# A two-expert gate that writes 67 MB: the first store is issued from GpSimd's queue instead of ScalarE's

## The chip, the core and the metric

The kernel runs on one core of a Trainium2 chip. The metric is the device time of one execution in microseconds (us), taken as the median of several runs. The core has compute engines that matter here in three roles: VectorE (DVE) does the arithmetic, ScalarE (ACT) two small activations, and SyncE (SP), ACT and GpSimd (POOL) can each issue transfers between the chip's memory and the on-chip tiles. The transfers themselves are carried by the core's 16 DMA engines, whoever issued them.

## The reference

```python
def reference(x, router_logits, k):          # x: 16 x 1024 x 512, logits: 16 x 1024 x 8, k = 2
    logits_max = np.max(router_logits, axis=-1, keepdims=True)
    probs = np.exp(router_logits - logits_max)
    probs = probs / np.sum(probs, axis=-1, keepdims=True)
    topk_indices = np.argsort(probs, axis=-1)[..., -k:]
    topk_probs = np.take_along_axis(probs, topk_indices, axis=-1)
    topk_probs = topk_probs / np.sum(topk_probs, axis=-1, keepdims=True)
    x_expanded = x[:, :, np.newaxis, :].repeat(k, axis=2)
    return (x_expanded * topk_probs[..., np.newaxis]).astype(np.float32)
```

For each of 16,384 tokens the two largest of eight logits give two weights that add to one, and the token's 512 numbers are written out twice, once times each weight. The input is 33.6 MB of x and 0.5 MB of logits, the output 67.1 MB.

## The kernel before

The tokens are split into two groups of 128 x 65 and 128 x 63 (`GROUPS`): each of the 128 partitions holds 65, then 63 rows, a row being one token's 512 float32 numbers (2 KB in, 4 KB out). Three tiles matter. `xs` holds the loaded rows of a group. `osp` has room for 18 output rows a partition, and before that serves as scratch for the weights. `WA` holds the two weights of every token.

`LOADS` cuts the loading of a group into transfers of 2, 4, 28 and 31 rows a partition (group 0) and 16, 16 and 31 (group 1). `STORES` lists, for each group, the stores as (first row, number of rows, tile, place in the tile). A store of place "osp" is computed into `osp`; a store of place "xs" overwrites `xs` in place, since two output rows' worth of loaded rows have been used up by then. For every store one DVE multiplication (line 138) makes the product. Where the place in `osp` is used a second time in the group (`again`), the product is cut in two: the first `FREE[g]` rows, which lie where an earlier and smaller store was, and the rest, which lie where a larger one was.

```python
LOADS = [[2, 4, 28, 31], [16, 16, 31]]
STORES = [
    [(0, 3, "osp", 0), (3, 15, "osp", 3), (18, 16, "xs", 0), (34, 15, "osp", 0), (49, 16, "xs", 33)],
    [(0, 16, "osp", 2), (16, 16, "xs", 0), (32, 15, "osp", 0), (47, 16, "xs", 32)],
]
FREE = [3, 2]
```

The early store of the title is the first entry, `(0, 3, "osp", 0)`: three rows a partition, 12 KB in one piece for each partition, made as soon as the weights are there. Its place, rows 0 to 2 of `osp`, is written again by the first part of the product for `(34, 15, "osp", 0)`, which must wait until the early store has been read out. Below, the stores of group 0 are called the early store, store 2, store 3, store 4 and store 5, in the order of the list.

All transfers but the early store are issued by SP (lines 122, 130, 131 and 151), in the order written, which `tc.keep_in_program_order` fixes. SP's queue therefore holds, in this order: the loads of 2 and 4 rows, the two pieces of the logits, the loads of 28 and 31 rows, stores 2 to 5, and then the loads and stores of group 1. Each store waits in SP's queue for its product. The early store alone stands on another queue, ACT's, which after the two activations (lines 37 and 38) has nothing else to do. Line 155 puts an empty instruction on SP that waits for all but the last transfer.

Of the kernel before, what the change touches and what calls it, by code (L numbers as in the profile page):

```python
# [1 line left out]

# [4 lines left out]

F32 = mybir.dt.float32
ALU = mybir.AluOpType
ACTF = mybir.ActivationFunctionType  # L10
P = 128


def top2_weights(nc, WA, dlt, room, logits, E):

    tt = nc.vector.tensor_tensor
    hi, lo, n = None, None, E  # L20
    while n > 1:
        n //= 2
        if hi is None:
            a, b = logits[:, :, 0:n], logits[:, :, n : 2 * n]
            nhi, nlo = room(n), b
            tt(nhi, a, b, op=ALU.max)  # L26
            tt(nlo, a, b, op=ALU.min)  # L27
        else:
            a, b = hi[:, :, 0:n], hi[:, :, n : 2 * n]
            nhi, nlo, tmp = room(n), room(n), room(n)  # L30
            tt(tmp, lo[:, :, 0:n], lo[:, :, n : 2 * n], op=ALU.max)  # L31
            tt(nlo, a, b, op=ALU.min)  # L32
            tt(nlo, nlo, tmp, op=ALU.max)  # L33
            tt(nhi, a, b, op=ALU.max)  # L34
        hi, lo = nhi, nlo
    tt(dlt, hi[:, :, 0], lo[:, :, 0], op=ALU.subtract)  # L36
    nc.scalar.activation(WA[:, :, 0], dlt, ACTF.Sigmoid, scale=-1.0)  # L37
    return nc.scalar.activation(WA[:, :, 1], dlt, ACTF.Sigmoid, scale=1.0)  # L38

GROUPS = [65, 63]

LOADS = [[2, 4, 28, 31], [16, 16, 31]]
BASE = [0, 1]
# [6 lines that stand above are left out]
L = 18  # L52

FREE = [3, 2]


@with_exitstack
def kernel(
    ctx: ExitStack,
    tc: tile.TileContext,  # L60
    x: bass.AP,
    router_logits: bass.AP,
    k: bass.AP,
    out: bass.AP,
):
    nc = tc.nc
    B, S, D = x.shape
    E = router_logits.shape[-1]
    N = B * S
    assert int(k) == 2 and E == 8 and N == P * sum(GROUPS)  # L70
    M = N // P

    x_v, o_v, rl_v = [], [], []
    t0 = 0
    for n in GROUPS:
        t1 = t0 + P * n
        x_v.append(
            x.rearrange("b s d -> (b s) d")[t0:t1].rearrange("(p m) d -> p m d", p=P)
        )
        o_v.append(  # L80
            out.rearrange("b s k d -> (b s) k d")[t0:t1].rearrange(
                "(p m) k d -> p m k d", p=P
            )
        )
        rl_v.append(
            router_logits.rearrange("b s e -> (b s) e")[t0:t1].rearrange(
                "(p m) e -> p m e", p=P
            )
        )
        t0 = t1  # L90

    wpool = ctx.enter_context(tc.tile_pool(name="wpool", bufs=1))
    xs = wpool.tile([P, max(GROUPS), D], F32)
    osp = wpool.tile([P, L, 2, D], F32)
    WA = wpool.tile([P, M, 2], F32)
    dlt = wpool.tile([P, M], F32)


    flat = osp.rearrange("p l k d -> p (l k d)")
    taken = [0]  # L100

    def room(n):
        o = taken[0]
        taken[0] += M * n
        return flat[:, o : o + M * n].rearrange("p (m n) -> p m n", n=n)

    logits = room(E)

    def place(where, at, n):

        if where == "osp":
            return osp[:, at : at + n]
        return xs[:, at : at + 2 * n, :].rearrange("p (r k) d -> p r k d", k=2)

    moved = []
    m0 = 0
    for g, G in enumerate(GROUPS):
        x0, r = BASE[g], 0
        for n in LOADS[g]:
            moved.append(  # L120
                tc.keep_in_program_order(
                    nc.sync.dma_start(  # L122
                        xs[:, x0 + r : x0 + r + n, :], x_v[g][:, r : r + n, :]
                    )
                )
            )
            r += n
            if g == 0 and r == 6:
                n0 = GROUPS[0]
                tc.keep_in_program_order(nc.sync.dma_start(logits[:, :n0], rl_v[0]))  # L130
                tc.keep_in_program_order(nc.sync.dma_start(logits[:, n0:], rl_v[1]))  # L131
                weights = top2_weights(nc, WA, dlt, room, logits, E)
        assert r == G
        for r, n, where, at in STORES[g]:
            og = place(where, at, n)
            again = where == "osp" and at == 0 and r > 0
            for a, b in [(0, FREE[g]), (FREE[g], n)] if again else [(0, n)]:
                product = nc.vector.tensor_tensor(  # L138
                    og[:, a:b],
                    xs[:, x0 + r + a : x0 + r + b, :]  # L140
                    .unsqueeze(2)
                    .to_broadcast([P, b - a, 2, D]),
                    WA[:, m0 + r + a : m0 + r + b, :]
                    .unsqueeze(3)
                    .to_broadcast([P, b - a, 2, D]),
                    op=ALU.mult,
                )

            queue = nc.scalar if g == r == 0 else nc.sync
            moved.append(  # L150
                tc.keep_in_program_order(queue.dma_start(o_v[g][:, r : r + n], og))  # L151
            )
        m0 += G

    seen = tc.keep_in_program_order(nc.sync.nop())
    for ins in [weights, product] + moved[:-1]:
        tc.add_manual_dep(
            seen.ins,
            ins.ins.name,
            mybir.DependencyInfo(  # L160
                mybir.DependencyClass.Sync, mybir.DependencyReason.DATA
            ),
            reason="all but the last transfer is done",
        )


# [1 line left out]
_INS = ['x', 'router_logits', 'k']  # L168
_OUTS = [((16, 1024, 2, 512), 'float32')]

_NUMBERS = {'k': 2}


# [26 lines left out]
```

## Time and profile before

| what | us |
|---|---|
| runs | 240.18 median of 3 (239.93 to 241.43) |
| profiled execution, its own time | 241.36 |
| its span, first to last instruction | 239.6 |
| DVE busy | 141.9 |
| ACT busy | 1.8 |
| POOL busy | 0.2 |
| SP's queue (q1): packet time of the 16 DMA engines | 96.7% of the span |
| ACT's queue (q10): packet time of the 16 DMA engines | 1.5% of the span |

The profile comes as a page with sums and as views of the trace: the queues and their issues, the timeline, the chain of work that ended last, and the busy time in chosen stretches. A line of the timeline gives the start, the duration, the engine ("SPq" or "ACTq" is the issuing part of that engine), the source line, the operation, and what is written from what. In the issues, "us to landing" is the time from issue until the transfer's completion was signalled. The number of packets counts pieces that a DMA engine handles one after the other.

### The profile page before, as it was taken

The numbers are of one execution on the slowest core, as the hardware profiler recorded it, in microseconds if no ns is written. First come the engines' busy times: TensorE is split into PE (matmuls) and PEld (weight loads), VectorE is DVE, ScalarE is ACT, GpSimd is POOL, SyncE is SP. The second block draws the span as 40 slices with busy tenths as digits, with TensorE's granted clock in tenths as the row PEclk, the third lists the DMA queues.
The fourth block names the chain that finished last, engine by engine and source line by source line (L and its number), as shares of the span: only waits on it lengthen the run. The fifth ranks groups of instructions, "written<-read, shape, count | busy, mean of one in ns | idle before, by whom it ended". The sixth has DMA issues, their size and how long they took to land.

```text
span 239.6 us, 106 instructions
## 1 busy us (share of the span) xinstructions
DVE 141.9 (59%) x22; ACT 1.8 (1%) x3; POOL 0.2 (0%) x4
## 2 busy tenths in 40 slices
DVE  0560499999789999200000699999405999960000
ACT  2000000000000000000000000000000000000000
POOL 0000000000000000000000000000000000000000
DMA  7989998979989897999899999999999899898984
GB/s 253 528 373 483 427 415 376 493 339 492 481 372 492 383 482 339 482 437 449 361 421 438 438 438 498 435 419 471 405 405 471 372 503 442 380 492 360 514 350 186
DMA packets 2592, 101.19 MB, mean 422 GB/s; under 512 B 288, under 2 KB 416, under 8 KB 672
## 3 DMA queue, kind: packets, MB, share of 16 engines
q1 hardware_dynamic: 2448, 99.62, 96.7%
q10 hardware_dynamic: 144, 1.57, 1.5%
HBM read 34.08 MB, written 67.11 MB: 422 GB/s over the span
## 4 chain that ended last, share of the span: by engine, by line
DMA 48%; DVE 40%; SPq 1%; issue 0%; DVEq 0%
DMA xs<-in_x_dram 25%; DVE osp L138 25%; DMA out_dram<-osp 23%; DVE xs L138 14%; SPq L122 0%; SPq L131 0%; SPq L130 0%; SPq L151 0%; DVEq L138 0%
## 5 line engine op out<-in xcount | busy, mean ns | idle before, releaser
L138 DVE TENSOR_TENSOR osp<-xs,WA 128x3072 f32<-128x3072 f32 (+5 forms) x7 | 69.4, 9909 | 62.7 <-DMA xs<-in_x_dram 47.3
L138 DVE TENSOR_TENSOR xs<-xs,WA 128x16384 f32<-128x16384 f32 x4 | 68.9, 17224 | 0.1
L26 DVE TENSOR_TENSOR osp<-osp 128x512 f32<-128x512 f32 x1 | 0.7, 693 | 8.5 <-DMA osp<-in_router_logits_dram 8.5
L37 ACT ACT_TABLE_LOAD x1 | 1.3, 1283 | 0.7 <-PEq L181 0.7
L27 DVE TENSOR_TENSOR osp<-osp 128x512 f32<-128x512 f32 x1 | 0.7, 691 | 0.0
L32 DVE TENSOR_TENSOR osp<-osp 128x256 f32<-128x256 f32 (+1 forms) x2 | 0.7, 351 | 0.0
L31 DVE TENSOR_TENSOR osp<-osp 128x256 f32<-128x256 f32 (+1 forms) x2 | 0.7, 350 | 0.0
L34 DVE TENSOR_TENSOR osp<-osp 128x256 f32<-128x256 f32 (+1 forms) x2 | 0.7, 350 | 0.0
L33 DVE TENSOR_TENSOR osp<-osp 128x256 f32<-128x256 f32 (+1 forms) x2 | 0.7, 350 | 0.0
L37 ACT ACTIVATE WA<-dlt 128x128 f32<-128x128 f32 x1 | 0.3, 315 | 10.5 <-DVE dlt L36 10.5
L36 DVE TENSOR_TENSOR dlt<-osp 128x128 f32<-128x128 f32 x1 | 0.3, 292 | 0.0
L38 ACT ACTIVATE WA<-dlt 128x128 f32<-128x128 f32 x1 | 0.3, 297 | 0.0
L181 POOL MEMSET const-bfloat16-1.0<- 128x1 bf16 x1 | 0.1, 101 | 0.0
L181 POOL MEMSET const-uint8-127<- 128x1 uint8 x1 | 0.1, 101 | 0.0
L181 POOL MEMSET const-float32-0.0<- 128x1 f32 x1 | 0.1, 98 | 0.2 <-issue 0.2
L181 POOL MEMSET const-float32-1.0<- 128x1 f32 x1 | 0.1, 98 | 0.0
## 6 DMA issues: line engine op xcount, KB each, us to landing
out_dram<-osp SPq DMA_DIRECT2D x3, 7680.0 KB, 23.5
xs<-in_x_dram SPq DMA_DIRECT2D x2, 7936.0 KB, 42.2
xs<-in_x_dram SPq DMA_DIRECT2D x2, 4096.0 KB, 40.1
xs<-in_x_dram SPq DMA_DIRECT2D x1, 7168.0 KB, 24.8
out_dram<-osp ACTq DMA_DIRECT2D x1, 1536.0 KB, 26.6
xs<-in_x_dram SPq DMA_DIRECT2D x1, 1024.0 KB, 5.9
xs<-in_x_dram SPq DMA_DIRECT2D x1, 512.0 KB, 3.9
osp<-in_router_logits_dram SPq DMA_DIRECT2D x1, 260.0 KB, 6.2
```

The costliest lines, as they stand in the source:

```text
L26: tt(nhi, a, b, op=ALU.max)
L27: tt(nlo, a, b, op=ALU.min)
L31: tt(tmp, lo[:, :, 0:n], lo[:, :, n : 2 * n], op=ALU.max)
L32: tt(nlo, a, b, op=ALU.min)
L33: tt(nlo, nlo, tmp, op=ALU.max)
L34: tt(nhi, a, b, op=ALU.max)
L36: tt(dlt, hi[:, :, 0], lo[:, :, 0], op=ALU.subtract)
L37: nc.scalar.activation(WA[:, :, 0], dlt, ACTF.Sigmoid, scale=-1.0)
L38: return nc.scalar.activation(WA[:, :, 1], dlt, ACTF.Sigmoid, scale=1.0)
L138: product = nc.vector.tensor_tensor(og[:, a:b], xs[:, x0 + r + a : x0 + r + b, :] .unsqueeze(2) .to_broadcast([P, b - a, 2, D]), WA[:, m0 ...
L181: nc = _bacc.Bacc("TRN2", target_bir_lowering=False, num_devices=1)
```

## The change

The queue of the early store becomes GpSimd's. Everything else stays: the same bytes, the same shape of the transfer, and the same waits ahead of it (the product of line 138, and the two logits transfers).

```diff
-            queue = nc.scalar if g == r == 0 else nc.sync
+            queue = nc.gpsimd if g == r == 0 else nc.sync
             moved.append(
                 tc.keep_in_program_order(queue.dma_start(o_v[g][:, r : r + n], og))
             )
```

In the order of the built program one row leaves ACT (the transfer of 128 x 3072 numbers) and one row with the same waits enters POOL, behind POOL's four opening memsets and ahead of its closing ones. The rows of DVE and SP stand as before. The transfer's completion is counted on a semaphore of its own kind, so the other transfers' completion semaphores are numbered anew; the transfers that each instruction waits for are the same wherever the data needs them.

## The prediction

> **What bounds the kernel now.** I read the page's sums first, then the DMA queues, then stretches of time, then the timeline around the early store. The sums and the queues:
>
> ```profile
> span 239.6 us, 106 instructions
> DVE 141.9 (59%) x22; ACT 1.8 (1%) x3; POOL 0.2 (0%) x4
> q1 hardware_dynamic: 2448, 99.62, 96.7%
> q10 hardware_dynamic: 144, 1.57, 1.5%
> ```
>
> No compute engine comes near the span. The queues do: 96.7% and 1.5% of 16 engines' span make 98.2%, or 235.3 us of 239.6. SP's queue (q1) moves 99.62 MB in 96.7% of 239.6 us = 231.7 us, so 16 engines together carry 430 GB/s, and one carries 26.9. ACT's queue (q10) has 1.57 MB: 1.5% of 239.6, that is 3.6 us of all 16 engines. It is these 3.6 us that change their queue. The stretches show where the missing 4.3 us are (columns: DVE, ACT, POOL busy, clock, DMA share, GB/s; a packet is counted where it starts, so short stretches are ragged):
>
> ```profile
> 0.00:2.00 2.00, 0.00 (x0) 1.28 (x1) 0.20 (x4) 1.00 0.25 31
> 20.00:44.00 24.00, 16.55 (x2) 0.00 (x0) 0.00 (x0) 1.00 1.03 438
> 48.00:236.00 188.00, 114.19 (x9) 0.00 (x0) 0.00 (x0) 1.00 1.00 431
> 236.00:237.00 1.00, 0.00 (x0) 0.00 (x0) 0.00 (x0) 1.00 0.16 66
> 237.00:238.00 1.00, 0.00 (x0) 0.00 (x0) 0.00 (x0) 1.00 0.00 0
> ```
>
> The engines are full from 20 to 44 and from 48 to 236 (share 1.03 and 1.00); idle time lies only at the two ends. So the end is set by bytes, and a change shows only if it adds work to the DMA engines, or leaves them without work in between. For the second I need the timeline around the early store:
>
> ```profile
> 13.02 3.36 DVE L138 TENSOR_TENSOR osp<-xs,WA 128x3072 f32<-128x3072 f32 x1 [0.58 <-ACT WA L38]
> 16.40 0.37 ACTq L151 DMA_DIRECT2D out_dram<-osp  x1
> 27.42 16.16 DVE L138 TENSOR_TENSOR osp<-xs,WA 128x15360 f32<-128x15360 f32 x1 [11.04 <-DMA xs<-in_x_dram]
> 43.60 0.35 SPq L151 DMA_DIRECT2D out_dram<-osp  x1
> 43.61 17.22 DVE L138 TENSOR_TENSOR xs<-xs,WA 128x16384 f32<-128x16384 f32 x1
> 60.75 3.35 DVE L138 TENSOR_TENSOR osp<-xs,WA 128x3072 f32<-128x3072 f32 x1
> 67.08 12.96 DVE L138 TENSOR_TENSOR osp<-xs,WA 128x12288 f32<-128x12288 f32 x1 [2.98 <-DMA out_dram<-osp]
> 80.07 0.33 SPq L151 DMA_DIRECT2D out_dram<-osp  x1
> ```
>
> and the transfers that share its time (size, us from issue to landing), with two steps of the chain that ended last (start, us):
>
> ```profile
> xs<-in_x_dram SPq DMA_DIRECT2D x1, 512.0 KB, 3.9
> xs<-in_x_dram SPq DMA_DIRECT2D x1, 1024.0 KB, 5.9
> osp<-in_router_logits_dram SPq DMA_DIRECT2D x1, 260.0 KB, 6.2
> osp<-in_router_logits_dram SPq DMA_DIRECT2D x1, 252.0 KB, 6.4
> xs<-in_x_dram SPq DMA_DIRECT2D x1, 7168.0 KB, 24.8
> out_dram<-osp ACTq DMA_DIRECT2D x1, 1536.0 KB, 26.6
> 2.56 24.83 DMA xs<-in_x_dram
> 43.60 23.45 DMA out_dram<-osp
> ```
>
> The early store is issued at 16.40 and landed at 43.0, 26.6 us for 3.6 us of work: it takes turns with the loads. A partition's piece is 12 KB (1536 KB over 128), 0.46 us on one engine; a load's piece is 56 or 62 KB, 2.1 or 2.3 us. Eight pieces an engine, each paired with one of the loads, make 8 x 2.75 = 22 us; with a fixed cost of 2.7 us (the 512 KB load: 3.9 us, of which 1.2 at 430 GB/s) and up to one load piece at the start, 2.1, that is 26.8. The turns explain the 26.6.
>
> **The change part by part.** (1) Bytes. The same 1.57 MB go over the same 16 engines: nothing added, if the pieces stay 12 KB.
>
> (2) Issue. ACT loses an issue of 0.37 us, with nothing behind it; POOL gains one, with only its closing behind it. Neither sets the end. What POOL takes until the first piece moves is not in this trace. The nearest rows: not under the 0.37 us of ACT's issue; from above, the early store's landing has to slip by 24 us before it costs anything (rival C), so I bound the delay by what it does earlier. I take 1 to 3 us, from the 2.7 us fixed cost above.
>
> (3) The 28-row load, whose landing starts DVE at 27.42. Up to its end 512 + 1024 + 260 + 252 + 7168 = 9216 KB, or 9.44 MB, go through SP's queue: 21.9 us, from the first issue at 0.7 and with the fixed 2.7 us that gives 25.3. It landed at 2.56 + 24.83 = 27.39. The 2.1 us between are mostly early-store pieces that got in first, about four of eight. A later early store lets the load land up to 2.1 us sooner; an early store that goes through in one go puts the other half ahead, 1.6 us later. Store 2 then issues between 41.5 and 45.2.
>
> (4) Does that empty the queue? Store 2 has 7680 KB, 7.86 MB, 18.3 us; its chain step took 23.45. Less 18.3 and the fixed 2.7, 2.4 us were spent behind loads. So store 2 may come 2.4 us later before an engine runs dry, and (3) uses at most 1.6. Earlier issue only lengthens the queue. Cost: 0; without that cover, at most 1.6.
>
> One rule speaks against this change. The Trainium skill (SBUF — State Buffer, Who interferes with whom, and the box on the "DVE blocks DMA" trap before it) says that descriptors of a GpSimd-issued transfer are written by GpSimd's cores, and that they are locked out while DVE runs an operation in a two-port mode; it adds that `tensor_tensor`, the only kind DVE runs here, was not seen to do this. By it the sum would be the same as long as the descriptors are written while DVE idles, which the timeline allows for 11.04 us behind 16.38.
>
> (5) DMA engines. How an engine takes pieces listed by GpSimd no row shows. If it waits for the list with nothing else to carry, every engine loses time: from 0 (the list is there when its turn comes) to the fixed cost without the issue, 2.7 - 0.4 = 2.3 us, if paid once, and 18 us if paid for each of eight pieces. A gain is excluded: q10's pieces run at the same 27 GB/s as q1's. I take 0.3, near the bottom, because pieces listed one behind the other in SP's queue show no such gap (share 1.00).
>
> (6) The closing.
>
> ```profile
> L195 POOLq DRAIN  x3: 34/41/70, 0.7 to 239.3; - x3
> L195 POOLq EVENT_SEMAPHORE_RANGE_CLEAR  x1: 93/93/93, 239.2 to 239.2; - x1
> SPq L195 <- DMA out_dram<-xs: 19.2, 1, 19.2
> ```
>
> SP waits 19.2 us for the last store, and all else at the end is POOL's drains of 34 to 70 ns and a clear of 93 ns. The clear covers eight semaphores more, 18 for 10: 0.1 us from its own row.
>
> **Sum.** 239.6 + 0 + 0 + 0 + 0.3 + 0.1 = 240.0 of span, and with the 1.76 us around it (241.36 - 239.6) 241.8. The profiled execution lies 1.18 above the median of 240.18, so in the runs' measure I forecast 240.6. The ragged end explains that distance: after 237 no packet starts, yet SP is released only near 239, so some engine was one 64 KB piece (2.4 us) behind. An execution may have that or not; the runs spread from 239.93 to 241.43.
>
> **The rivals.** (A) The forecast, 240.6: bytes bound, the queue never dry.
>
> (B) The engines stall on GpSimd's lists, point (5) at a larger size. Paid at the beginning and once more at the completion: 2 x 2.3 = 4.6 less the 0.3 counted, 244.9. For it: a different producer of the list, of which this trace shows nothing. Against it: two queues already share the engines between 20 and 43 us at a share of 1.03.
>
> (C) The early store lands too late, which ends on the slower side. Place: DVE's three-row product at 60.75, which overwrites the early store's rows. It has 17.7 us in hand (60.75 - 43.0), then 2.98 us that DVE idles behind it anyway, then store 4's own distance behind other work:
>
> ```profile
> out_dram<-osp SPq DMA_DIRECT2D x1, 7680.0 KB, 24.4
> ```
>
> 24.4 - 18.3 - 2.7 = 3.4 us. So it decides from a landing at 60.75 + 2.98 + 3.4 = 67.1, 24.1 us later than now. Beyond that every microsecond goes into the end, since SP's queue holds nothing else until store 4 is ready. How could it be that late? If each 12 KB is listed as three 4 KB pieces, and one is taken per turn: 24 turns of 2.3 + 0.15 us, 59 us, plus 4.8, landing at 80. That costs 12.9 us: 253. Two pieces (16 turns, 61.7) cost nothing. Against it: all of q1's 2448 packets come from 17 transfers at 144 each, so a partition's row goes out whole whatever its size, up to 64 KB.
>
> A late list does the same. If POOL has not listed the pieces by 27.42 and cannot while DVE works, whose products follow each other until 60.8, the list starts there and the store lands 26.6 us on, near 87, 20 us past the point: 260. Against it stand the 11 us of idle DVE. The rule of the Trainium skill cited in (4) is what could hold POOL up like this.
>
> (D) Faster. Only the ends are idle, 4.3 us in all, and the change touches neither; even ending evenly would save some 1.5 us against the profiled execution and nothing against the fastest run.
>
> **How the numbers follow.** A change of 1%, 2.4 us, is about what a measurement of this kernel can tell from none: same means 237.8 to 242.6. A has 0.51, with its own range 239.5 to 242.4 (nothing, or one stall of 2.3 paid nearly whole). B has 0.26, nearly all of it over 242.6, since its price starts at 2.3; the new producer is the one thing here of which no row shows anything. C has 0.16, of which 0.03 by the late list, D 0.07, over half of it over 1%. So faster 0.04, same 0.54 (A and the rest of D), slower 0.42. The range reaches from 239.4 to 248.0: it holds A and most of B (three payments of 2.3 and the scatter of the runs) and leaves out C and D, 2 in 10. The likeliest is A, 240.6.
>
> **What would show it.** A new queue of 1.57 MB in 144 packets in place of q10, and 96.7% for q1, show (1); more packets there speak for C. The early store's landing between 25 and 46 shows (2); over 67, C. DVE's 16.16 us product starting between 25.3 and 29.1 shows (3); store 2 issued before 46 and a DMA share of 1.00 from 44 on, (4). A packet share of the new queue well over 1.5%, or engines idle between 17 and 48, shows B. DVE waiting at 60.8 for the early store, and a hole in the DMA share near 85, would be C. The prediction is wrong if SP's queue runs dry anywhere, or if all transfers behind the early store land later by the same amount.

## The result, and the profile after

| kernel | median us (range, runs) | against before, 95% interval |
|---|---|---|
| before | 240.11 (239.91 to 241.43, 7) | |
| after | 241.99 (239.78 to 242.61, 7) | 1.0065 [1.0045, 1.0085] |

By the ratio the change costs 0.65%, 1.6 us; the medians lie 1.88 us apart. That stays within the 1% called "same" in the prediction and is clear of zero. The runs of after scatter more than those of before: one is at 239.78, two are near 241.3, four are between 242.0 and 242.6.

The profiled execution of after took 242.61 us, its span is 240.8. The profiled execution of before, 241.36 us, lies well over its median too, so the two profiles are 1.25 us apart, less than the medians. The page's sums and queues:

```profile
span 240.8 us, 105 instructions
DVE 141.9 (59%) x22; ACT 1.8 (1%) x3; POOL 0.9 (0%) x5
q1 hardware_dynamic: 2448, 99.62, 96.2%
q0 software_dynamic: 144, 1.57, 1.5%
```

A queue q0, "software", has taken the place of q10, with the same 144 packets, the same bytes and the same 1.5%. SP's queue moves the same bytes in 96.2% of 240.8, 231.6 us, as before (231.7). The DMA engines do no more work than they did. The timeline around the early store, and the transfer's landing:

```profile
16.59 0.66 POOL L151 DMA_DIRECT2D out_dram<-osp  x1 [16.15 <-DVE osp L138]
27.86 16.16 DVE L138 TENSOR_TENSOR osp<-xs,WA 128x15360 f32<-128x15360 f32 x1 [11.57 <-DMA xs<-in_x_dram]
44.05 0.35 SPq L151 DMA_DIRECT2D out_dram<-osp  x1
...
67.90 12.96 DVE L138 TENSOR_TENSOR osp<-xs,WA 128x12288 f32<-128x12288 f32 x1 [3.35 <-DMA out_dram<-osp]
...
out_dram<-osp POOLq DMA_DIRECT2D x1, 1536.0 KB, 26.6
```

POOL takes 0.66 us where ACT took 0.37, and the early store lands after the same 26.6 us. DVE's next product starts 0.44 us later than before, store 2 with it, and the product behind store 2 0.82 us later. The stretches say whether that emptied a queue:

```profile
20.00:44.00 24.00, 16.14 (x1) 0.00 (x0) 0.00 (x0) 1.00 1.04 438
48.00:236.00 188.00, 114.63 (x9) 0.00 (x0) 0.00 (x0) 1.00 1.00 431
236.00:237.00 1.00, 0.00 (x0) 0.00 (x0) 0.00 (x0) 1.00 0.01 0
237.00:238.00 1.00, 0.00 (x0) 0.00 (x0) 0.00 (x0) 1.00 0.15 66
```

It did not: the share stays at 1.00. What moved is a single piece at the end. 66 GB/s over 1 us is 66 KB, one 64 KB piece of the last store. Before, that piece started between 236 and 237; now it starts between 237 and 238, when everything else has been sent. The packets that the traces keep, each with its start and duration, say the same: fifteen engines have sent their last piece by 236.95 before and by 236.89 after, and the sixteenth at 238.47 before and at 239.67 after. Between these two executions the whole loss is the lateness of one engine of sixteen, which is late in both.

Where does it fall behind? The packets that start between 20 and 22 us, by queue (packets, MB, share of 16 engines in the stretch), before:

```profile
q1 hardware_dynamic: 16, 0.92, 108.9%
q10 hardware_dynamic: 14, 0.17, 20.1%
```

and after:

```profile
q1 hardware_dynamic: 16, 0.92, 110.1%
q0 software_dynamic: 1, 0.01, 1.4%
```

Before, fourteen engines take their first early-store piece in this stretch. After, a single engine does; the other fifteen take theirs after 22 us, behind one more load piece:

```profile
q1 hardware_dynamic: 13, 0.75, 208.8%
q0 software_dynamic: 15, 0.18, 43.1%
```

(the stretch from 22 to 23 us of after). The one engine is the one that stands furthest behind: the fifteen begin another load piece between 20.02 and 20.47, and the late one becomes free at 20.62 and takes a store piece. So the store's pieces became available between these times. The late engine carries a store piece of 0.46 us ahead of its load piece, which the others do not. (Before, the picture is less clean: two engines begin a load piece at 20.16 and 20.20, between others that take store pieces from 20.01 on, so the moment is not quite the same for all sixteen.)

Later its lateness grows. Only one packet starts between 24 and 24.5, one between 46 and 46.5, and one between 160 and 160.1 of after:

```profile
q1 hardware_dynamic: 1, 0.06, 37.4%
...
q1 hardware_dynamic: 1, 0.06, 39.6%
...
q1 hardware_dynamic: 1, 0.06, 223.2%
```

A share times 16 engines times the stretch is the piece's duration: 2.99, 3.17 and 3.57 us, for load pieces of 56 and 62 KB that take 2.1 and 2.34 at the engine's usual pace. They are the late engine's last pieces of a load, under way while the other engines have begun store pieces. The same three of before (23.8 to 24, 45.5 to 46, 159 to 159.5):

```profile
q1 hardware_dynamic: 1, 0.06, 83.8%
...
q1 hardware_dynamic: 1, 0.06, 36.0%
...
q1 hardware_dynamic: 1, 0.06, 40.3%
```

are 2.68, 2.88 and 3.22 us: stretched too, each by 0.3 less.

How late the last engine is can be followed through the packets: the end of its last piece of a transfer, less the middle of the sixteen engines' ends, in us. Two profiles of the experiments below stand beside before and after, e2 (239.68 us) and e5 (241.91 us):

| after the end of | before | after | e2 | e5 (two engines) |
|---|---|---|---|---|
| the 4-row load | 0.5 | 0.4 | 0.4 | 0.3 |
| the 28-row load | 0.8 | 1.6 | 0.1 | 1.2 |
| the 31-row load, stores follow | 1.1 | 2.0 | 0.1 | 1.6 |
| store 5, loads follow | 1.1 | 2.0 | 0.1 | 1.6 |
| the last load of group 1, stores follow | 2.0 | 3.1 | 0.2 | 2.4 |
| the last store | 2.0 | 3.1 | 0.2 | 2.4 |
| span | 239.6 | 240.8 | 237.9 | 240.1 |

The spans differ as the last lateness does, to 0.1 us. Where it grows, it grows while loads and stores run side by side, in the turns with the early store and at the changes to the next stores; through a row of stores it stays as it is. The turn's 0.46 us is not simply added to it: every engine has eight pieces of the early store, in whatever order. And a turn ahead is not the only way to be late: the late engine of before took its first store piece in the same stretch as thirteen others.

### The profile page after: what moved, and what is told of

Read it like the earlier page. It is cut to its first block, busy times and chain, and to the rows that moved or that the text cites. A ratio compares the mean times of both kernels' runs of the same rounds, so it can differ in the third digit from the quotient of the medians.

```text
span 240.8 us, 105 instructions
## 1 busy us (share of the span) xinstructions
DVE 141.9 (59%) x22; ACT 1.8 (1%) x3; POOL 0.9 (0%) x5
## 3 DMA queue, kind: packets, MB, share of 16 engines
q1 hardware_dynamic: 2448, 99.62, 96.2%
## 4 chain that ended last, share of the span: by engine, by line
DMA 48%; DVE 39%; SPq 1%; issue 0%; DVEq 0%
DMA xs<-in_x_dram 25%; DVE osp L138 25%; DMA out_dram<-osp 23%; DVE xs L138 14%; SPq L122 0%; SPq L131 0%; SPq L130 0%; SPq L151 0%; DVEq L138 0%
## 5 line engine op out<-in xcount | busy, mean ns | idle before, releaser
L151 POOL DMA_DIRECT2D out_dram<-osp x1 | 0.7, 657 | 16.1 <-DVE osp L138 16.1
## 6 DMA issues: line engine op xcount, KB each, us to landing
out_dram<-osp SPq DMA_DIRECT2D x3, 7680.0 KB, 23.8
out_dram<-osp POOLq DMA_DIRECT2D x1, 1536.0 KB, 26.6
```

## The experiments

Theory A (turns): the price hangs on the moment at which the early store's pieces become available to sixteen engines that stand at slightly different points of their load pieces. If the moment falls between them, the late ones get a store piece a turn ahead of the others. Theory B (the list): pieces listed by GpSimd cost an engine time, whatever the moment.

To move the moment without touching the transfer, VectorE computes part of the early product a second time, with the same values, in the 11 us in which it is idle anyway (the edit is shortened; `...` stands for what is left out):

```diff
+            if g == r == 0:
+                nc.vector.tensor_tensor(og[:, 2:3, 0:1], ...the same operands..., op=ALU.mult)   # 512 numbers: e1, e2
             queue = ...                                   # nc.scalar: e1, e7; nc.gpsimd: e2, e3, e5, e6
```

with 1024 numbers in e3 and e7, 1920 in e5 and 2544 in e6. e4 takes `queue = nc.sync`.

> The early store stays on ACT's queue as in the kernel before, but VectorE computes a sixth of its product a second time (512 numbers a partition, about 0.6 us, while VectorE would idle), so the store is issued about 0.6 us later. Theory A (turns): the time depends only on the moment at which the store's pieces become available to the 16 engines, which stand at different points of their load pieces; 0.6 us later is the moment at which GpSimd's store became available, and the one late engine takes its store piece a turn ahead of the others; about 241.5 to 242.2 us, and between 20 and 22 us one or a few q10 pieces start instead of fourteen. Theory B (the list): pieces listed by GpSimd cost an engine time whatever the moment; here nothing is listed by GpSimd, so 240.1 us as before.

> The changed kernel, the early store on GpSimd's queue, with the same second computation of a sixth of the product, so the store is issued about 0.6 us later than in the changed kernel. Theory A (turns): the pieces become available near 21.2 us, when every engine is inside its seventh load piece, so all take their first store piece in the same turn and no engine falls behind: 239.7 to 240.3 us. Theory B (the list): 242.0 us as in the changed kernel.

> The changed kernel with a third of the product computed twice (1024 numbers a partition, about 1.15 us), so the store is issued about 1.15 us later. Theory A (turns): available near 21.7 us, still inside everybody's seventh load piece: 239.7 to 240.3 us. Theory B (the list): 242.0 us.

> The early store goes over SP's own queue, behind the loads, so no engine ever chooses between two queues. Theory A (turns): no engine is set back by a piece from another queue, and only the lateness from the first loads is left: 239.3 to 240.0 us. Theory B (the list): no software list, 240.1 us as before; a time clearly under 240 speaks for A, a time of 241 or more against both.

> The changed kernel with 1920 numbers a partition of the early product computed twice, so the store is issued about 2.1 us later than in the changed kernel: one load piece's time, 2.12 us. Theory A (turns) says that the price comes back with the period of a load piece: the availability again falls between the fifteen engines' piece ends and the late one's, 241.0 to 242.5 us. A rival (any delay over 0.6 us avoids the early part of the loads and is good for ever): 239.7 to 240.3 us, as with 0.7 and 1.2 us of delay.

> The changed kernel with 2544 numbers a partition computed twice, the store issued about 2.8 us later: one load piece's time and the 0.7 us that were free of charge. Theory A (turns): again inside everybody's piece, 239.7 to 240.3 us. The rival gives the same, so this run only tells whether the price of a delay rises steadily (it would be above e5) or comes and goes.

> The early store on ACT's queue, issued about 1.2 us later than in the kernel before (a third of the product computed twice). Theory A (turns): past the moment that cost 0.5% at a delay of 0.55 us, inside everybody's load piece: 239.7 to 240.3 us. A rival (on ACT's queue a later store costs more, steadily): over 241.2 us.

Issue times are those of each kernel's own profile; 12 runs each, 7 of after.

| kernel | queue | issued at | median us (range) | against before |
|---|---|---|---|---|
| before, beside e1 to e4 | ACT | 16.40 | 240.02 (239.60 to 241.35), 35 runs | |
| before, beside e5 to e7 | ACT | 16.40 | 239.89 (239.61 to 241.42), 29 runs | |
| e1 | ACT | 16.94 | 241.23 (239.95 to 242.79) | 1.0051 [1.0025, 1.0077] |
| e7 | ACT | 17.50 | 239.91 (239.60 to 240.51) | 0.9995 [0.9980, 1.0009] |
| after | POOL | 16.59 | 241.99 (239.78 to 242.61) | 1.0065 [1.0045, 1.0085] |
| e2 | POOL | 17.33 | 239.95 (239.68 to 240.29) | 0.9994 [0.9981, 1.0007] |
| e3 | POOL | 17.83 | 240.03 (239.68 to 240.80) | 0.9997 [0.9987, 1.0007] |
| e5 | POOL | 18.77 | 241.64 (239.90 to 242.31) | 1.0048 [1.0024, 1.0071] |
| e6 | POOL | 19.45 | 240.02 (239.81 to 240.23) | 0.9997 [0.9983, 1.0011] |
| e4 | SP, behind the loads | 16.29 | 240.27 (240.04 to 240.52) | 1.0009 [1.0001, 1.0017] |

B falls three times: GpSimd's queue shows no price in e2, e3 and e6 (the intervals leave room for 0.3 us at most), and ACT's queue has one in e1 without GpSimd. The additional product is not the cause: e1 and e2 make the same one, and only e1 is slower. A holds: the price is there at 16.59, gone at 17.33 and 17.83, back at 18.77, 2.18 us later, where a load piece takes 2.12, and gone again at 19.45. So neither a price that rises with the delay nor "any delay is enough" fits. e2's packets show the clean case, none of q0 between 20 and 22, and all sixteen between 22 and 23:

```profile
q1 hardware_dynamic: 16, 0.92, 108.3%
...
q1 hardware_dynamic: 11, 0.63, 173.8%
q0 software_dynamic: 16, 0.20, 46.0%
```

and e5's the other: two engines a turn ahead between 22 and 24, most others between 24 and 25:

```profile
q1 hardware_dynamic: 16, 0.92, 127.1%
q0 software_dynamic: 2, 0.02, 2.9%
...
q0 software_dynamic: 12, 0.15, 34.5%
```

and two late 64 KB pieces at its end, 131 GB/s, where e2 has none:

```profile
236.00:237.00 1.00, 0.00 (x0) 0.00 (x0) 0.00 (x0) 1.00 0.31 131
```

The profile of e1 is of its shortest execution (239.95 us). It shows the clean case on ACT's queue: no q10 piece starts between 20 and 22, sixteen do between 22 and 23, and no late piece is left at the end. No row shows the turn ahead on ACT's queue, so for e1's longer executions the cause is read from its times. The wide ranges of after, e1 and e5, against the narrow ones of the others, fit a moment at an edge: between the last engine that began a load piece and the first late one lie 0.15 us in after (20.47 to 20.62) and 0.18 in e5 (22.54 to 22.72).

e4 missed its expectation: without turns the time is 0.25 us over before's 240.02, not under it.

The second part of the story, that lateness grows, was tried with an additional transfer on SP's queue in e4's kernel. It reads 28 KB for each of two partitions into a place that is free then, and the numbers are not used (the edits are shortened):

```diff
+    nc.sync.dma_start(osp[0:2, 10:17] as 14 rows, x_v[0][0:2, 0:14, :])   # e8: behind the logits; e9: ahead of the loads of group 1
+    nc.sync.dma_start(xs[0:2, 0:14, :], x_v[0][0:2, 0:14, :])             # e10: ahead of the last store
```

> The early store on SP's queue (no turns, 240.27 us) and one more transfer on SP's queue behind the logits: 28 KB for each of two partitions, 57 KB in all, read into a part of the tile that is free then and never used. If two partitions go to two engines, these two are 1.06 us late from the start. Theory A with growth (a late engine's last load piece runs slowly once the others have gone on to stores, so its lateness grows at every change from loads to stores): the end moves by more than 1.06 us, to 241.9 to 243.5. Rival (lateness is carried along and does not grow): 241.2 to 241.5. If the transfer is spread over all 16 engines: no change, 240.3 to 240.5.

> The early store on SP's queue, and the additional transfer of 57 KB for two partitions (read into a free part of the tile, not used) stands in SP's queue ahead of the loads of group 1, so two engines become 1.06 us late between store 5 and those loads, with one change from loads to stores still to come. Theory (lateness grows at a change from loads to stores, as 1.11 grew to 1.98 and 1.93 to 3.08 us in the two profiles): 242.0 to 242.5 us, about 1.9 over the 240.27 without the transfer. Rival (lateness is only carried, and the 2.3 us of the first trial were the price of the transfer at its place): the end moves by the bytes, 1.06 to 1.3 us, to 241.3 to 241.6.

> The same additional transfer ahead of the last store, where no change from loads to stores follows (it is read into rows of the tile that have been stored). Both theories: the bytes alone, 1.06 to 1.3 us over 240.27: 241.3 to 241.6. A time near 242.5 would say that the transfer itself costs over 2 us wherever it stands, and that the first trial showed no growth.

| place of the additional 57 KB | changes from loads to stores still to come | median us (range, runs) | over e4 (240.27) |
|---|---|---|---|
| e8: behind the logits | 2 | 242.55 (242.44 to 242.64, 5) | 2.28 |
| e9: ahead of group 1's loads | 1 | 242.38 (242.13 to 242.79, 4) | 2.11 |
| e10: ahead of the last store | 0 | 241.49 (241.34 to 241.50, 4) | 1.22 |

e4 was timed earlier, beside a before of 240.02; beside e8 before stood at 239.89 and beside e9 and e10 at 239.84, so the last column may be up to 0.2 us too small.

Two engines are late in e8, as the two 64 KB pieces (131 GB/s) that start when the others are through show:

```profile
236.00:237.00 1.00, 0.00 (x0) 0.00 (x0) 0.00 (x0) 1.00 0.01 0
237.00:238.00 1.00, 0.00 (x0) 0.00 (x0) 0.00 (x0) 1.00 0.30 131
```

At the end the two pieces cost 1.2 to 1.4 us, little more than their bytes, which are 1.06 us by the engine's pace. With one change from loads to stores still to come they cost nearly twice that, but e8, with two changes ahead, is hardly above e9. The packets say where the time arises. The rows below have the last load pieces of the late engines, 62 KB and 2.34 us at the usual pace: in e8 at the first change (42 to 43 us, two pieces) and at the second (161.14 to 161.25, one of the two), and in e9 at its only change (160.4 to 160.555, two pieces):

```profile
q1 hardware_dynamic: 2, 0.13, 48.9%
...
q1 hardware_dynamic: 1, 0.06, 133.1%
...
q1 hardware_dynamic: 2, 0.13, 218.3%
```

These are 3.91 us each on average, 2.34, and 2.71 on average. In e8 the lateness, read as in the table above, grows from 1.8 to 2.8 at the first change and stays at 2.8 at the second. In e9 it is 2.0 already ahead of group 1's last load, since the additional pieces took 1.5 us each and the load pieces behind them 1.6 and 1.7 for 1.2; after the change it is 2.2. So most of what e9 costs over e10 arises among the loads and not at the change: the rival of e9's expectation, a price of the place, holds in part. The first change of e8, and the table above, show a growth; the second change of e8 shows none. Why a late engine's load piece slows down while others store, and why it sometimes does not, stays open; it was not tried further.

## Why the prediction was right, and where its sum was not

The measured 241.99 lies in the range, and "same" was the likeliest case. That it lies within A's own range too, 239.5 to 242.4, is in part luck: that range made room for a stall of 2.3 us on GpSimd's list, which does not exist, and the 1.6 us came from elsewhere. By its points:

(1) Bytes: right, q0's row is q10's row.

(2) Issue: 0.66 us on POOL for 0.37, off the path. From issue to the first piece it took 4.0 us (16.59 to 20.62), with ACT at most 3.6 (16.40 to 20.01), not 1 to 3. The moment does matter, though not as the prediction thought: e1 shows that 0.54 us of delay on ACT's own queue costs nearly as much, 1.2 us by the ratio.

(3) and (4) The 28-row load, store 2 and the queue: store 2 issued at 44.05 (41.5 to 45.2 forecast), and the share stayed at 1.00. Right, cost 0. The bound without turns was good: in e4 no store stands among the first loads, and DVE's product starts at 25.30, for the 25.3 of the prediction. The reading of the 2.1 us was not: about two early-store pieces an engine, 0.9 us, went ahead of the last pieces of the 28-row load, not four, and the load pieces beside them took up to 2.68 us for 2.12. And the later store let most engines end that load sooner, as (3) says (the middle of them at 25.45 for 25.77), but its landing was set by the late one, at 27.03 for 26.57.

The rule on the "DVE blocks DMA" trap (the Trainium skill, SBUF — State Buffer, SBUF: two separate sides) was no threat here: POOL's operation ended at 17.25, 10.6 us before DVE's next. No run here issues the store while DVE works, so none tests that rule. Another rule would have had it differently: the Trainium skill (DMA: Bandwidth & Descriptors, Queues, rings and completion order) says that an engine drains a whole packet, typically 9 to 17 descriptors, from one queue before it switches. By it, if an engine's eight pieces made one packet, they would have gone through in one go, 8 x 0.46 = 3.7 us, an estimate. This trace does not agree: it shows one piece a turn, from 20.62 on, and a landing at 43.2.

(5) The DMA engines: this is the step that was wrong. The prediction sought a cost in how an engine takes GpSimd's list and put 0.3 us for it; e2, e3 and e6 measure nothing (0.9994 to 0.9997). The cost there is instead, 1.6 us by the ratio, is one engine's lateness. The prediction saw the ragged end, took 1.18 us for it off the sum, and wrote: "An execution may have that or not". It was the one quantity that the change moves. The sum's own result, 0.4 us over before, was thus a quarter of the measured 1.6.

(6) The closing: the clear took 136 ns for 93, beside a POOL drain of 88 ns:

```profile
L195 POOLq DRAIN  x3: 34/88/26719, 16.6 to 240.6; - x3
L195 POOLq EVENT_SEMAPHORE_RANGE_CLEAR  x1: 136/136/136, 240.4 to 240.4; - x1
```

Under 0.1 us, as put. (The long drain begins at 16.6 and is POOL waiting out its own transfer; nothing waits for it.)

The rivals: (B) had the right sign for a wrong reason, the stall on the list does not exist here. (C) was far off: the early store landed at 43.2, 24 us before its point. (D): one run of after, at 239.78, was under before's fastest in the first seven, 239.91. It is no gain: e2, e3, e6 and e7 lie at this level, and before itself has runs down to 239.60. That this run had the clean turn is not shown, since its packets were not kept.

## What to carry to other kernels

When DMA engines are full from end to end, look at which engine ends last, not only at their mean: one late engine out of sixteen is 6% of a stretch's share and all of the end. A transfer on a second queue, issued into the middle of a large one, can set a few engines a turn apart, and whether it does hangs on a few tenths of a microsecond; a queue change, or a slightly longer instruction ahead, may show as a cost that has nothing to do with the queue. Before blaming the queue, shift the issue by half a piece and by a whole piece: a price that goes and comes back is a matter of phase.

## What the runs showed of the hardware that was not expected

A store issued from GpSimd's queue took turns with SP's loads piece by piece, as one from ACT's queue did (26.6 us to landing in both). The price of its moment came back after 2.18 us, one load piece. Lateness of single engines grew over most changes from loads to stores and stayed as it was through rows of stores: in after from 2.0 to 3.1 us at the second change, where the late engine's last load piece took 3.57 us for 2.34. In e8 it grew at the first change and not at the second. 57 KB on two engines, 1.06 us each by the usual pace, cost 1.22 us ahead of the last store and 2.11 ahead of a group's loads.
